# Six column orders for the up products of the third expert in a two-layer hybrid block with a mixture of experts

## The chip, the cores and the metric

The kernel runs on one core of one Trainium2 chip. The metric is the device time of one execution in microseconds (us); the median over the runs is what counts. Beside it there is one profiled execution, whose trace is read below. PE is TensorE (PEld its weight loads), DVE VectorE, ACT ScalarE, POOL GpSimd, SP SyncE, whose queue issues the loads.

## The reference, cut to what matters

Two layers of a mixer (gated convolution and chunkwise retention) and a feed-forward part, on 256 tokens of 1024 features. In the first layer the feed-forward part is dense, in the second it is a mixture of eight experts, two for each token, with 3584 inner features. The change is in the experts:

```python
def expert_block(args):
    xe, e = args
    a = xe @ w1[e]
    c = xe @ w3[e]
    return (jax.nn.silu(a) * c) @ w2[e]
```

All arrays are float32.

## The kernel before

After the mixer of the second layer the kernel gathers, for each expert, up to 128 of its tokens (a loop behind a condition serves more) and runs through the weights of all eight experts, 56 blocks in all: expert `e` from 0 to 7, and in it block `b` from 0 to 6, each block 512 of the 3584 inner features. The third expert is `e == 2`.

The float32 products are made of three products each. `parts` (L106 to L110) splits a weight half of 128 partitions x 1024 columns into a rounded high part `wh` (ACT, L109) and the remainder `wl` (DVE or POOL, L110); the tokens are split likewise (`gah` and `gal` for the third expert). `mm3` (L152 to L156) issues the three matmuls high by high (L154), high by low (L155) and low by high (L156), all into the same PSUM tile. Its first operand, the tokens, is loaded into the array (128 x 128, a weight load on PEld); its second, the weights of the expert, streams through as 512 columns, and the 512 results of each partition go to one bank of PSUM.

In a block the up products come first: four calls of `up` make `a` (the product with w1) and four more make `cc` (with w3). One call takes a half unit of weights, views it as two pieces of 512 columns, and calls `mm3` for each. So a block has 8 x 2 x 3 = 48 up matmuls: 24 into one tile `ac`, 24 into another. Between them stand the four transposes of the block before (`ph`, L816) and, in some blocks, small matmuls that gather tokens (`pg`) or scatter results (`pc`). Behind the up products come 24 down matmuls of the block before (`y`). `act` (L806 to L811) reads the two `ac` tiles, in plain order, in the next block.

The weights come through SP's queue in pieces of 1 MB (`raw`, L132), which wait for a free buffer; ACT and DVE split them into four pairs of `wh` and `wl`, which in turn come free when PE has used them. On each engine the instructions run in the order in which the program issues them.

Of the kernel before, what the change touches and what calls it, by code (L numbers as in the profile page):

```python
# [74 lines left out]
def tile_hybrid(ctx: ExitStack, tc, xT_in, x_in, ws, wm, cols, lnp, gnp, router, ident_in, rot, mask_in, out):  # L75
    nc = tc.nc
    v, sc, pe, gp = nc.vector, nc.scalar, nc.tensor, nc.gpsimd
    A = slice(None)
# [22 lines left out]
    def half(h):  # L101
        return slice(512 * h, 512 * h + 512)
# [43 lines left out]
    W = Stream(emit)  # L146
# [5 lines left out]
    def mm3(o, a, b, first, last):  # L152

        pe.matmul(o, a[0], b[0], start=first, stop=False, skip_group_check=True)  # L154
        pe.matmul(o, a[0], b[1], start=False, stop=False, skip_group_check=True)  # L155
        pe.matmul(o, a[1], b[0], start=False, stop=last, skip_group_check=True)  # L156

    def two(p, *idx):
        return (p[0][idx], p[1][idx])

    def view(p, pattern, **kw):
        return [w.rearrange(pattern, **kw) for w in p]


    for l in range(DEPTH):
        b = l * MIXU
# [60 lines left out]
    for q in range(4):  # L227
        k = slice(2 * q, 2 * q + 2)
# [489 lines left out]
    def bc(a):  # L718
        return a.unsqueeze(2).to_broadcast([128, NT, NE])
# [69 lines left out]
    def start_acc():  # L789

        for t in range(NT):
            for h in range(2):
                o = acc[:, t, half(h)]
                sc.mul(o, f32(xn[0][:, t, half(h)]), ALPHA)
                v.scalar_tensor_tensor(o, f32(xn[1][:, t, half(h)]), ALPHA, o, op0=ALU.mult, op1=ALU.add)
                yield

    def up(p, q, w, G):

        w = view(w, "p (k f) -> p k f", k=2)  # L800
        for k in range(2):
            mm3(p, two(G, A, 2 * q + k), two(w, A, k), q == 0 and k == 0, q == 3 and k == 1)

    def new_ac():
        return pac.tile([128, 512], F32, tag="ac", name="ac")

    def act(a, cc):
        hh = mo2.tile([128, 512], F32, tag="hh", name="hh")
        sc.activation(hh, a, AF.Silu)
        v.tensor_tensor(hh, cc, hh, op=ALU.mult)  # L810
        return hh  # L811

    def turn(hh):
        p = ptp.tile([128, 4, 128], F32, tag="tp", name="ph")
        for j in range(4):
            pe.transpose(p[:, j, :], hh[:, 128 * j:128 * j + 128], ident)  # L816
        return p

    def split_h(p):
        return split([128, 4, 128], p, mo2, "ht")  # L820
# [8 lines left out]
    got = {}  # L829
# [9 lines left out]
    def later_tokens(e0):  # L839
        g = tokens_of(e0)  # L840
        yield
        yield
        yield from g
# [20 lines left out]
    def step():  # L864
        while side:
            if next(side[0], 0) is None:
                return
            side.pop(0)
# [3 lines left out]
    def down_prev(last):  # L872
        nonlocal y, hT
        hp = hT
        pe_, pb, _ = prev
        if pb == 0:
            y = new_y()
        for q in range(4):
            down(hp, q, W.take(), y, pb == 0, pb == NB - 1)
            if q == 0:  # L880
                step()
            if last and q == 1:
                hT = [raw2[1 + i].tile([128, 4, 128], F32R, tag="raw", name="htl") for i in range(2)]
                parts(hT[0], hT[1], turn(hh))
        if pb == NB - 1:
            side.append(combine(y, got[pe_][1], lambda t: gate[:, t, pe_:pe_ + 1]))

    for e, b in blocks:
        if e == 0 and b == 1:
            W.look = LOOK  # L890
        if e == 1 and b == 0:
            assert main not in seq
            once.release()
            acc = main.tile([128, NT, D], F32, tag="x", name="acc")
            side.append(start_acc())
            late.append(ctx.enter_context(tc.tile_pool(name="late", bufs=1, reuse_waits="tile")))
        if e == 0 and b == 2:

            g = mo.tile([128, 4, NT], F32, name="g")
            v.tensor_tensor(g[:, 0], m2, m1, op=ALU.subtract)  # L900
            sc.activation(g[:, 1], g[:, 0], AF.Exp)
            v.tensor_scalar(g[:, 0], g[:, 1], 1.0, None, op0=ALU.add)
            v.reciprocal(g[:, 2], g[:, 0])
            v.tensor_tensor(g[:, 3], g[:, 1], g[:, 2], op=ALU.mult)
            gate = mo.tile([128, NT, NE], F32, name="gate")
            v.tensor_tensor(gate, s1, bc(g[:, 2]), op=ALU.mult)
            v.tensor_tensor(s2, s2, bc(g[:, 3]), op=ALU.mult)
            v.tensor_tensor(gate, gate, s2, op=ALU.add)
        if e % 2 == 1 and b == 2 and e + 1 < NE:
            side.append(later_tokens(e + 1))  # L910
        a = new_ac()
        for q in range(4):
            up(a, q, W.take(), got[e][0])
            if not prev:
                next(g0, 0), next(g0, 0)
            if prev and q == 0:
                hh = act(*prev[2])
            if prev and q == 2:
                hp = turn(hh)
            if prev and q == 3:  # L920
                hT = split_h(hp)
        step()
        cc = new_ac()
        for q in range(4):
            up(cc, q, W.take(), got[e][0])
            if q < 3:
                step()
        step()
        if prev:
            last = (e, b) == blocks[-1]  # L930
            if last:
                hh = act(a, cc)
            down_prev(last)
        prev = (e, b, (a, cc))
# [22 lines left out]
    for h in range(2):  # L957
        for t in range(NT):
            o = acc[:, t, half(h)]
# [20 lines left out]
    if GENERAL:  # L980
        most = nc.values_load(cnti[0:1, 0:1], min_val=0, max_val=S)
        with tc.If(most > WIN):
            rk2 = mo.tile([128, NT, NE], F32, name="rk2")
            v.tensor_scalar(rk2, rk, -float(WIN), None, op0=ALU.add)
            with tc.For_i(0, NE, 1) as e:
                rc = mo.tile([128, NT, 2], F32, name="rc")
                for t in range(NT):
                    v.tensor_copy(rc[:, t, 0:1], rk2[:, t, ds(e, 1)])
                    v.tensor_copy(rc[:, t, 1:2], gate[:, t, ds(e, 1)])
                gg = gather(lambda i, t: rc[:, t, 0:1], 1, ((mo, "ga"),), mo)  # L990
                gs, PT = next(gg)
                run(gg)
                yy = new_y()
                for b in range(NB):
                    def src(i):
                        return wm[ds(e, 1), 6 * b + i].rearrange("o p f -> (o p) f")

                    def both(i):
                        s = Unit(src(i))
                        return [emit("first", s), emit("second", s)]  # L1000

                    ac = [new_ac(), new_ac()]
                    for i in range(4):
                        for j, w in enumerate(both(i)):
                            up(ac[i // 2], 2 * (i % 2) + j, w, gs[0])
                    hT = split_h(turn(act(*ac)))
                    for i in range(2):
                        for j, w in enumerate(both(4 + i)):
                            down(hT, 2 * i + j, w, yy, b == 0, b == NB - 1)
                run(combine(yy, PT[:, 0, :], lambda t: rc[:, t, 1:2]))  # L1010
# [5 lines left out]
    for t in (1, 0):  # L1016
        for h in range(2):
            o = acc[:, t, half(h)]
            v.scalar_tensor_tensor(o, o, mv[:, t, 0:1], gt[:, 0, half(h)], op0=ALU.subtract, op1=ALU.mult)  # L1019
    for t, h in ((1, 0), (1, 1), (0, 0), (0, 1)):  # L1020
        o = acc[:, t, half(h)]
# [92 lines left out]
```

## Time and profile before

| what | value |
|---|---|
| median of the runs | 1468.6 us (two runs, 1467.22 and 1469.97) |
| the profiled execution | 1474.45 us, its span 1472.6 us |
| granted PE clock, mean | 0.986 |
| PE busy | 1436.3 us, 98% of the span |
| DVE busy | 1226.3 us, 83% |
| ACT busy | 973.6 us, 66% |
| DMA | 77.5% of 16 engines' span, 295 GB/s of reads and writes |

The span is what the trace covers, and 1.85 us lie around it. A busy share counts an instruction from its start to its end, and matmuls overlap: one of 512 columns is drawn 0.39 us long, but the next starts after some 0.23 us. So PE's time is read from the distance between starts.

### The profile page before, as it was taken

The page shows a single profiled execution, that of the slowest core. Times are in us where ns is not written, and L with a number is a line of the kernel's source. Part 1 is how long each engine was busy: PE and PEld are TensorE (multiplying, and loading weights), DVE is VectorE, ACT ScalarE, POOL GpSimd, SP SyncE. Part 2 cuts the span into 40 slices and gives each one's busy share as a digit, 9 for nine tenths or more (in the row PEclk, how much of TensorE's full clock was granted, in tenths as well). Part 3 has the DMA queues.
Part 4 walks back from the last instruction along what each step waited for, and adds up shares of the span by engine and source line. Part 5 has one row for each costly group of instructions (what it writes and reads, how often), then busy time and mean ns, then how long its engine had stood idle before and what let it go on. Part 6 is the DMA issues. An engine that isn't in the chain of part 4 may idle for free. (4 is left out here: it accounts for less than half of the span.)

```text
span 1472.6 us, 19730 instructions
## 1 busy us (share of the span) xinstructions
PE 1436.3 (98%) x7385; PEld 1211.4 (82%) x7385; DVE 1226.3 (83%) x1405; ACT 973.6 (66%) x1155; POOL 269.6 (18%) x136
## 2 busy tenths in 40 slices
PE   9999999999997999999999999999999999999995
PEld 8859999999866888888888888888888888888884
DVE  7976545547996799999999998999999899999996
ACT  6324444443524787877778777887887777778773
POOL 5630000001844111111111111111111111111111
PEclk9999999999997999999999999999999999999998
DMA  9535454454637879998999998999999899999951
GB/s 367 215 115 217 183 195 178 180 192 160 219 114 286 344 283 361 369 356 341 378 356 378 365 359 332 365 364 372 378 367 346 336 374 352 375 367 369 369 209 60
DMA packets 62311, 436.10 MB, mean 296 GB/s; under 512 B 7040, under 2 KB 7424, under 8 KB 9856
## 3 DMA queue, kind: packets, MB, share of 16 engines
q1 hardware_dynamic: 61920, 434.24, 77.5%
q8 instruction: 60, 0.98, 0.3%
q10 hardware_dynamic: 288, 0.52, 0.1%
q14 instruction: 43, 0.35, 0.1%
HBM read 433.69 MB, written 1.05 MB: 295 GB/s over the span
## 5 line engine op out<-in xcount | busy, mean ns | idle before, releaser
L110 DVE TENSOR_TENSOR wl<-raw,wh 128x1024 fp32r<-128x1024 f32 (+1 forms) x704 | 880.0, 1285 | 60.6 <-ACT wh L109 37.3
L109 ACT CAST wh<-raw 128x1024 fp32r<-128x1024 f32 (+1 forms) x802 | 822.0, 1046 | 155.1 <-PE ac L156 90.0
L110 POOL TENSOR_TENSOR wl<-raw,wh 128x1024 fp32r<-128x1024 f32 x98 | 242.3, 2488 | 1095.1 <-ACT wh L109 1019.4
L154 PE MATMUL ac<-wh,gah 128*128 128x512 f32 x448 | 177.4, 396 | 0.0
L155 PE MATMUL ac<-wl,gah 128*128 128x512 f32 x448 | 174.9, 390 | 0.5 <-POOL wl L110 0.5
L156 PE MATMUL ac<-wh,gal 128*128 128x512 f32 x448 | 175.0, 391 | 0.0
L156 PE MATMUL y<-wh,htl 128*128 128x512 f32 x448 | 174.4, 389 | 0.0
L155 PE MATMUL y<-wl,hth 128*128 128x512 f32 x440 | 171.7, 390 | 0.1
L154 PE MATMUL y<-wh,hth 128*128 128x512 f32 x440 | 171.4, 389 | 0.0
L154 PE MATMUL wk<-xh,wh 128*128 128x256 f32 x512 | 145.6, 284 | 0.7 <-ACT wh L109 0.7
L156 PE MATMUL wk<-xh,wl 128*128 128x256 f32 x512 | 145.1, 283 | 0.0
L155 PE MATMUL wk<-xl,wh 128*128 128x256 f32 x512 | 144.9, 283 | 0.0
L391 DVE SCALAR_TENSOR_TENSOR wk<-u,colt,wk 128x256 f32<-128x256 f32 x209 | 99.8, 488 | 5.7
L156 PEld LDWEIGHTS wk<-xh,wl 128*128 128x128 f32 x512 | 99.2, 194 | 0.5 <-DVE wl L110 0.5
L154 PEld LDWEIGHTS wk<-xh,wh 128*128 128x128 f32 x512 | 97.5, 190 | 2.4 <-ACT wh L109 1.3
L155 PEld LDWEIGHTS ac<-wl,gah 128*128 128x128 f32 x448 | 84.4, 188 | 17.7 <-POOL wl L110 0.9
L156 PEld LDWEIGHTS ac<-wh,gal 128*128 128x128 f32 x448 | 84.2, 188 | 17.9
L155 PEld LDWEIGHTS wk<-xl,wh 128*128 128x128 f32 x512 | 97.6, 191 | 0.9
L156 PEld LDWEIGHTS y<-wh,htl 128*128 128x128 f32 x448 | 84.1, 188 | 17.4
L154 PEld LDWEIGHTS ac<-wh,gah 128*128 128x128 f32 x448 | 84.5, 189 | 16.6
L155 PEld LDWEIGHTS y<-wl,hth 128*128 128x128 f32 x440 | 82.6, 188 | 18.8 <-DVE wl L110 1.9
L154 PEld LDWEIGHTS y<-wh,hth 128*128 128x128 f32 x440 | 82.6, 188 | 17.1
(202 smaller groups left out, 2049.6 us busy)
## 6 DMA issues: line engine op xcount, KB each, us to landing
raw<-in_wm_dram SPq DMA_DIRECT2D x336, 1024.0 KB, 6.6
raw<-in_ws_dram SPq DMA_DIRECT2D x68, 1024.0 KB, 4.9
raw<-in_lnp_dram SPq DMA_DIRECT2D x4, 1024.0 KB, 4.6
raw<-in_ws_dram SPq DMA_DIRECT2D x8, 256.0 KB, 5.7
xf<-in_xT_dram SPq DMA_DIRECT2D x4, 256.0 KB, 4.9
x<-in_x_dram SPq DMA_DIRECT2D x1, 1024.0 KB, 7.4
mask<-in_mask_dram SPq DMA_DIRECT2D x1, 768.0 KB, 12.1
gn<-in_gnp_dram SPq DMA_DIRECT2D x2, 256.0 KB, 8.3
```

The costliest lines, as they stand in the source:

```text
L109: sc.copy(hi, src)
L110: (eng or v).tensor_tensor(lo, src, f32(hi), op=ALU.subtract)
L154: pe.matmul(o, a[0], b[0], start=first, stop=False, skip_group_check=True)
L155: pe.matmul(o, a[0], b[1], start=False, stop=False, skip_group_check=True)
L156: pe.matmul(o, a[1], b[0], start=False, stop=last, skip_group_check=True)
L391: v.scalar_tensor_tensor(d, u[:, cc, k:k + S], w[:, k:k + 1], o, op0=ALU.mult, op1=ALU.add)
```

## The change

In blocks 1 to 6 of the third expert the streamed operand and the PSUM output of all 48 up matmuls are addressed through the same rearranged pattern. Each column still meets its own place in PSUM, so the tile `ac` holds what it held; only the order in time in which the 512 columns pass is another. Block 0 and all other experts keep the plain order.

```diff
+    walks = (None, ("p (a b i) -> p b a i", dict(a=2, i=2)), ("p (a b i) -> p b a i", dict(a=32, i=2)),
+             ("p (c a i) -> p a c i", dict(a=2, i=16)), ("p (a i) -> p a i", dict(a=4)),
+             ("p (a b i) -> p b a i", dict(a=2, i=16)), ("p (a b i) -> p b a i", dict(a=4, i=4)))
+
+    def walk(o, n):
+
+        return o.rearrange(walks[n][0], **walks[n][1]) if walks[n] else o
+
-    def up(p, q, w, G):
+    def up(p, q, w, G, n=0):
 
         w = view(w, "p (k f) -> p k f", k=2)
         for k in range(2):
-            mm3(p, two(G, A, 2 * q + k), two(w, A, k), q == 0 and k == 0, q == 3 and k == 1)
+            mm3(walk(p, n), two(G, A, 2 * q + k), [walk(o, n) for o in two(w, A, k)], q == 0 and k == 0, q == 3 and k == 1)
...
-            up(a, q, W.take(), got[e][0])
+            up(a, q, W.take(), got[e][0], b if e == 2 else 0)
...
-            up(cc, q, W.take(), got[e][0])
+            up(cc, q, W.take(), got[e][0], b if e == 2 else 0)
```

The six orders, in columns of 4 bytes:

| block | shape of the walk | adjoining columns in a row | from there it goes | stretches in 512 columns |
|---|---|---|---|---|
| 1 | 128 x 2 x 2 | 2 | to and fro between the two halves, 256 columns apart | 256 |
| 2 | 8 x 32 x 2 | 2 | 16 columns on from the last start | 256 |
| 3 | 2 x 16 x 16 | 16 | 32 columns on, then once more for the other half of each 32 | 32 |
| 4 | 4 x 128 | 512 | nowhere: this is the plain order | 1 |
| 5 | 16 x 2 x 16 | 16 | to and fro between the two halves | 32 |
| 6 | 32 x 4 x 4 | 4 | 128 columns on, four such places in turn | 128 |

No instruction is added, removed or moved. On PE, where the down products `y` of block 0's turn end and the up products of block 1 begin, the kernel before has these rows:

```order
L155 MATMUL y<-wl,hth 128x512
L156 MATMUL y<-wh,htl 128x512
L154 MATMUL ac<-wh,gah 128x512
L155 MATMUL ac<-wl,gah 128x512
L156 MATMUL ac<-wh,gal 128x512
```

and the changed one these:

```order
L155 MATMUL y<-wl,hth 128x512
L156 MATMUL y<-wh,htl 128x512
L154 MATMUL ac<-wh,gah 128x128x2x2
L155 MATMUL ac<-wl,gah 128x128x2x2
L156 MATMUL ac<-wh,gal 128x128x2x2
```

The shapes (partitions first, then the walk) are all that differs. The same holds in blocks 2, 3, 5 and 6 with the shapes of the table. In block 4 PE's rows in the changed kernel are those of before, the four pieces of 128 columns having been merged into one run of 512:

```order
L155 MATMUL y<-wl,hth 128x512
L156 MATMUL y<-wh,htl 128x512
L154 MATMUL ac<-wh,gah 128x512
L155 MATMUL ac<-wl,gah 128x512
L156 MATMUL ac<-wh,gal 128x512
```

So five blocks of 48 matmuls, 240 in all, have another order.

## Rows read from the trace of the kernel before

**Rows 1.** The profile's page: the span, the engines' busy time, slices in tenths
```profile
span 1472.6 us, 19730 instructions
PE 1436.3 (98%) x7385; PEld 1211.4 (82%) x7385; DVE 1226.3 (83%) x1405; ACT 973.6 (66%) x1155; POOL 269.6 (18%) x136
PE   9999999999997999999999999999999999999995
PEclk9999999999997999999999999999999999999998
```

**Rows 2.** Busy time by stretch: expert 3's blocks 1 to 6, one row each
```profile
core 0: us, PE busy (x) PEld busy (x) DVE busy (x) ACT busy (x) POOL busy (x), PEclk, DMA share, GB/s
737.26:754.98 17.72, 17.72 (x82) 14.66 (x80) 17.05 (x17) 14.18 (x17) 2.40 (x1) 1.00 0.90 331
754.98:772.68 17.70, 17.70 (x82) 14.66 (x80) 16.74 (x16) 13.39 (x15) 2.50 (x1) 1.00 0.96 376
772.68:789.49 16.81, 16.81 (x77) 13.90 (x76) 15.27 (x13) 13.40 (x15) 2.42 (x1) 1.00 0.96 376
789.49:806.28 16.79, 16.79 (x77) 13.91 (x76) 15.26 (x13) 13.39 (x15) 2.42 (x1) 1.00 0.94 375
806.28:823.10 16.82, 16.82 (x78) 13.91 (x76) 15.26 (x13) 13.41 (x15) 2.41 (x1) 1.00 0.95 373
823.10:839.89 16.79, 16.79 (x77) 13.91 (x76) 15.26 (x13) 13.40 (x15) 2.42 (x1) 1.00 0.96 376
```

**Rows 3.** Waits in expert 3 (720.47 to 839.89): us in total, times, longest
```profile
POOL wl L110 <- ACT wh L109: 102.5, 7, 15.3
ACT wh L109 <- PE ac L156: 12.8, 40, 0.8
ACT wh L109 <- PE y L156: 6.9, 21, 0.8
```

**Rows 4.** The same stretch, SP's queue of loads
```profile
SPq L132 <- DVE wl L110: 104.8, 43, 3.7
```

**Rows 5.** Timeline of PE, block 5's up products: start, length, instruction
```profile
806.28 0.39 PE L154 MATMUL ac<-wh,gah 128*128 128x512 f32 x1
806.51 0.39 PE L155 MATMUL ac<-wl,gah 128*128 128x512 f32 x1
...
810.14 0.39 PE L156 MATMUL ac<-wh,gal 128*128 128x512 f32 x1
810.37 0.60 PE L816 MATMUL ph<-ident,hh 128*128 128x128 f32 x4
810.72 0.48 PE L154 MATMUL ac<-wh,gah 128*128 128x512 f32 x1
```

**Rows 6.** Timeline of PE, products of 256 columns in the dense layer
```profile
199.75 0.28 PE L154 MATMUL wk<-xh,wh 128*128 128x256 f32 x1
...
203.52 0.28 PE L156 MATMUL wk<-xh,wl 128*128 128x256 f32 x1
```

**Rows 7.** Timeline of PE, the first up products of the first expert
```profile
479.69 0.63 PE L154 MATMUL ac<-wh,gah 128*128 128x512 f32 x1
480.11 0.63 PE L155 MATMUL ac<-wl,gah 128*128 128x512 f32 x1
480.54 0.63 PE L156 MATMUL ac<-wh,gal 128*128 128x512 f32 x1
480.97 0.47 PE L154 MATMUL ac<-wh,gah 128*128 128x512 f32 x1
```

**Rows 8.** Busy time by stretch: the three matmuls ahead of 480.97 us
```profile
479.69:480.97 1.28, 1.28 (x5) 0.99 (x5) 0.70 (x2) 0.56 (x2) 0.00 (x0) 0.50 0.98 416
```

**Rows 9.** Groups by line, shapes apart: count, busy us, mean ns, idle before
```profile
L421 DVE TENSOR_TENSOR u<-wk,sgl 128x256 f32<-128x256 f32 x8 | 3.4, 419 | 3.3 <-ACT sgl L420 3.3
L441 DVE TENSOR_TENSOR t<-wk,rott 128x256 f32<-128x256 f32 x8 | 3.0, 414 | 0.0
L110 DVE TENSOR_TENSOR wl<-raw,wh 128x1024 fp32r<-128x1024 f32 x692 | 872.2, 1295 | 59.2 <-ACT wh L109 35.9
L109 ACT CAST wh<-raw 128x1024 fp32r<-128x1024 f32 x790 | 815.2, 1052 | 153.3 <-PE ac L156 90.0 <-PE y L156 48.7 <-PE wk L156 12.3
```

## The prediction, made before the changed kernel ran

> **What bounds the kernel now.** I began with the page: PE is busy 98% of the span and its row of tenths falls below 9 only around the start of the experts and in the last slice, and the clock's row with it [rows 1]. A busy share proves little for matmuls that overlap, so I looked at the six blocks by stretch: PE has work in every microsecond of all of them, at a granted clock of 1.00 [rows 2]. Next, who waits for whom in this expert: ACT's splitting waits for PE to give back weights, POOL waits for ACT, SP's queue of loads waits 104.8 us for buffers that the splitting gives back, and no row has PE waiting for anything [rows 3, 4]. So the weights are there before PE wants them; the feed follows PE, not the reverse, though DMA at a share of 0.90 to 0.96 is near its own limit. Last, PE's timeline: in block 5 the starts of 18 up matmuls go from 806.28 to 810.14 us, 17 steps of 0.2271 us each, and after the four transposes the next 30 follow at the same pace [rows 5]. PE sets the time here and nothing behind it is slack: a microsecond that an up matmul gains or loses is a microsecond of the kernel.
>
> **The change part by part.** Nothing is moved, added or waited for anew. Weight loads are the same instructions, the tile `ac` has the same content, and its readers read it in plain order. Blocks 0 and 4 are as before. What is left is one question: how long 512 columns take in five orders, for 48 matmuls each.
>
> What a column costs in plain order comes from two rows. Products of 256 columns start 32 steps apart between 199.75 and 203.52 us, 0.1178 us each [rows 6]. From 256 to 512 columns the step grows by 0.1093 us, that is 0.427 ns a column, and some 8 ns of a step are fixed.
>
> The trace has no matmul whose streamed operand or output hops, so the price is bounded from both sides.
>
> *From below:* a walk cannot stream faster than one column at a time, so a gain could come from the fixed 8 ns alone, 240 x 8 ns = 1.9 us; nothing in the change touches them, and I take 0.
>
> *From above, for a walk at half pace:* at a granted clock of 0.50 [rows 8], the lower of the two levels (1.2 GHz), the first three up matmuls of the first expert start 0.4267 us apart, (480.97 - 479.69) / 3 [rows 7]. That is 512 columns at half pace, and 0.1996 us more than at 1.00. For the five orders together: 240 x 0.1996 = 47.9 us.
>
> Which of the five pay? The nearest row with hops is on DVE: L441 (in `rotary`) reads PSUM and writes its result in pieces of 32 elements with 32 left out between them, and takes 414 ns for 256 elements, against 419 ns for L421, which reads and writes in one run [rows 9]. Hops between long pieces are free there. But DVE and ACT are slow readers: 1295 ns and 1052 ns for 1024 elements, 1.26 and 1.03 ns each [rows 9], while PE draws one every 0.427 ns, two and a half to three times as many. What hides a hop there may not here. And 16 adjoining columns (walks 3 and 5, one hop in 6.8 ns) are near that row, 2 adjoining columns (walks 1 and 2, one hop in 0.85 ns) are far from it; 4 (walk 6, one in 1.7 ns) lie between.
>
> I think of it as a fetch that brings a few adjoining columns at once at a steady rate that the plain order just uses up. Nothing here shows how many. If two, every walk is free. If four, walks 1 and 2 need twice the fetches (256 for 128) and run at half pace, the others are untouched. If eight, they run at a quarter and walk 6 at half. I take four: the plain order needs no more than one fetch in 1.7 ns then, close to the 1.03 to 1.26 ns at which the other engines take even a single element, while two would mean a fetch in 0.85 ns, faster than any row shows.
>
> **The sum.** 96 matmuls (walks 1 and 2) x 0.1996 us = 19.2 us. The profiled execution would go from 1474.45 to 1493.6 us (its span from 1472.6 to 1491.8). The median of the runs lies 5.85 us below that execution, so I forecast 1468.6 + 19.2 = 1487.8 us, 1.3% longer. Nothing gives it back: the loads were already waiting for buffers, so a slower PE lets no work run ahead that PE later saves.
>
> [...]
>
> **The rivals.**
>
> *All walks are free* (fetches of two columns, or more fetches at hand than the plain order uses): 1468.6 us, not slower. For it speaks L441; against it that PE draws 2.5 times as fast. It decides wherever the extra is under 0.03 us a matmul.
>
> *Any stepped pattern runs at half pace,* long pieces too, for instance because the output side takes two results at once only in plain order: 240 x 0.1996 = 47.9 us, 1516.5 us, 3.3% slower. Against it speaks L441 for the reading; for writing to PSUM at this pace no row speaks at all. The line to slower by over 2% (29.4 us) lies at 29.4 / 240 = 0.122 us a matmul if all five pay alike, or 0.306 us if walks 1 and 2 pay alone. [...]
>
> *Short pieces cost far more* (fetches of eight columns): walks 1 and 2 at a quarter pace take twice the 0.4267 us of half pace [rows 7], 0.8534 - 0.2271 = 0.6263 us more than now, times 96 that is 60.1 us; walk 6 at half pace adds 48 x 0.1996 = 9.6 us: 1468.6 + 69.7 = 1538.3 us. Against it: a fetch would then take 3.4 ns, while ACT takes single elements in 1.03 ns each [rows 9].
>
> *Faster:* 1.9 us at most, so not by 2%.
>
> **How the numbers follow.** The likeliest, walks 1 and 2 at about half pace, has 0.38; its own range is 1478 (only one of them pays, 9.6 us) to 1498 (a third order or a second hop cost joins, 28.8 us). All free has 0.35. All five at half pace has 0.13, far more for short pieces 0.12, and 0.02 is left for a time a little below that of before. The range takes in the first three: 1465 us (the free case less the 1.9 us and the 1 to 2 us by which the runs differ) to 1517 us, leaving out the dear short pieces, 0.12, and what is left. About 2% is what a measurement of this kernel can tell from no change. Slower by over 2%: 0.13 + 0.12 and 0.02 from the upper edge of the likeliest, 0.27. Within 2%: 0.72. Faster: 0.01.
>
> **What would show it.** In the trace after, each block is its own experiment. Steps between starts of `ac` matmuls: 0.227 us in blocks 0 and 4; 0.43 us in blocks 1 and 2, which then last 17.7 + 9.6 = 27.3 us; 0.227 us in blocks 3, 5 and 6, which stay at 16.8 us. ACT's waits for PE `ac` grow by about what PE loses, the granted clock stays at 1.00, and no row of PE waiting appears. A step of 0.227 us in blocks 1 and 2 makes the first rival true; over 0.3 us in block 3 or 5 makes the second; 0.6 us and more in block 1 or 2 the third. A cost in one of blocks 1 and 2 alone would mean that the distance of the hop counts, not only the length of the piece. What makes the forecast wrong is the choice of four columns a fetch, which no row settles.

## The result and the profile after

The changed kernel takes 1487.6 us (two runs, 1487.18 and 1488.02) against 1468.6 us: 1.0131 times the time before, with a 95% interval of 1.0107 to 1.0156. That is 19.0 us more, where 19.2 were forecast. The sum came out, in part by luck: of its terms one was 4.5 us too high, and three that it put at nothing make 3.2 us.

The profile's page of the changed kernel, with the lines that answer to [rows 1]:

```profile
span 1485.4 us, 19726 instructions
PE 1448.2 (97%) x7385; PEld 1207.8 (81%) x7385; DVE 1227.4 (83%) x1405; ACT 974.0 (66%) x1155; POOL 269.3 (18%) x136
PEclk9999999999998999999999999999999999999998
```

Nothing in it tells what happened: PE's share is a point lower, the clock is where it was. The stretches tell it. These are the six blocks of expert 3, as in [rows 2] (stretch, its length, then busy time of PE, PEld, DVE, ACT, POOL, granted clock, DMA share, GB/s):

```profile
732.04:754.88 22.84, 22.84 (x81) 15.08 (x80) 18.10 (x17) 14.36 (x17) 2.39 (x1) 1.00 0.80 288
754.88:782.45 27.57, 27.57 (x81) 15.52 (x80) 17.09 (x15) 13.45 (x15) 2.39 (x1) 1.00 0.62 222
782.45:799.84 17.39, 17.39 (x78) 13.94 (x76) 15.44 (x13) 13.38 (x15) 2.40 (x1) 1.00 0.95 357
799.84:816.64 16.80, 16.80 (x78) 13.91 (x76) 15.25 (x13) 13.40 (x15) 2.41 (x1) 1.00 0.95 368
816.64:834.09 17.45, 17.45 (x78) 14.02 (x77) 15.44 (x13) 13.39 (x15) 2.40 (x1) 1.00 0.97 374
834.09:852.87 18.78, 18.78 (x78) 14.24 (x77) 15.49 (x13) 13.71 (x15) 2.36 (x1) 1.00 0.90 335
```

Against 17.72, 17.70, 16.81, 16.79, 16.82 and 16.79 us before [rows 2], the blocks grew by 5.12, 9.87, 0.58, 0.01, 0.63 and 1.99 us, 18.20 in all. (The medians, of two runs each, differ by 19.0; the runs of the kernel before alone lie 2.75 us apart.) PE is busy in every microsecond of them, and the clock stays at 1.00. Behind block 6 both profiled executions run alike: 1485.4 - 852.87 = 632.5 us here, 1472.6 - 839.89 = 632.7 before. Ahead of block 1 this execution was 5.2 us quicker (732.04 for 737.26), in parts that the change doesn't touch; that is why the spans differ by 12.8 only and the medians by 19.0.

The timeline of PE gives the step, from the first to the 18th `ac` matmul of a block (17 steps), here of blocks 1, 2, 3 and 6:

```profile
732.04 0.50 PE L154 MATMUL ac<-wh,gah 128*128 128x512 f32 x1
...
737.80 0.52 PE L156 MATMUL ac<-wh,gal 128*128 128x512 f32 x1
...
754.88 0.59 PE L154 MATMUL ac<-wh,gah 128*128 128x512 f32 x1
...
762.20 0.62 PE L156 MATMUL ac<-wh,gal 128*128 128x512 f32 x1
...
782.45 0.41 PE L154 MATMUL ac<-wh,gah 128*128 128x512 f32 x1
...
786.54 0.40 PE L156 MATMUL ac<-wh,gal 128*128 128x512 f32 x1
...
834.09 0.43 PE L154 MATMUL ac<-wh,gah 128*128 128x512 f32 x1
...
838.64 0.44 PE L156 MATMUL ac<-wh,gal 128*128 128x512 f32 x1
```

That is 0.3388, 0.4306, 0.2406 and 0.2676 us, and 0.2400 in block 5, against 0.2265 in block 4, which keeps the plain order. All steps below are read in this way.

The waits of expert 3 from its block 0 on (715 to 852.87 us; us in total, times, longest) show where a slower PE is felt, as in [rows 3]:

```profile
POOL wl L110 <- ACT wh L109: 118.8, 7, 25.2
ACT wh L109 <- PE ac L156: 28.0, 43, 2.0
```

ACT waits 28.0 us for PE to release weights, 12.8 before; PE itself still has no row of waiting for the feed there.

### The profile page after: what moved, and what is told of

The parts are those of the page before. It is cut to its first block, busy times and chain, and to the rows that moved or that the text cites. A ratio compares the mean times of both kernels' runs of the same rounds, so it can differ in the third digit from the quotient of the medians.

```text
span 1485.4 us, 19726 instructions
## 1 busy us (share of the span) xinstructions
PE 1448.2 (97%) x7385; PEld 1207.8 (81%) x7385; DVE 1227.4 (83%) x1405; ACT 974.0 (66%) x1155; POOL 269.3 (18%) x136
## 5 line engine op out<-in xcount | busy, mean ns | idle before, releaser
L154 PE MATMUL ac<-wh,gah 128*128 128x512 f32 x448 | 183.5, 410 | 0.0
L155 PE MATMUL ac<-wl,gah 128*128 128x512 f32 x448 | 181.2, 404 | 0.5 <-POOL wl L110 0.5
L156 PE MATMUL ac<-wh,gal 128*128 128x512 f32 x448 | 181.4, 405 | 0.0
```

## The experiments

The first question was which side pays, the reading of the streamed operand or the writing of PSUM; the next which property of an order sets the price; the last whether an order can be quicker than the plain one.

**The operand alone.** `up` walks the operand as in the change and writes the output plainly. The table of walks has an entry for each block, first the operand's walk, then the output's (from the edit against the kernel before):

```diff
+    walks = {(2, 1): ((2, 2), None), (2, 2): ((32, 2), None), (2, 3): (("step", 2, 16), None), (2, 5): ((2, 16), None), (2, 6): ((4, 4), None)}
...
+            mm3(walk(p, n[1]), two(G, A, 2 * q + k), [walk(o, n[0]) for o in two(w, A, k)], q == 0 and k == 0, q == 3 and k == 1)
```

> The five walks on the streamed operand alone; the output is written in plain order, so in these five blocks the columns of a and cc change places and all else is as before. Theory O (the cost is in reading the streamed operand from SBUF): the steps between starts stay those of the changed kernel, 0.333 us in block 1, 0.431 in block 2, 0.241 in blocks 3 and 5, 0.268 in block 6; expert 3's blocks 1 to 6 last 120.8 us and the kernel some 1487.6 us, 1.3% over the one before. Theory P (the cost is in writing PSUM): all steps 0.227 us, 102.6 us, 1468.6 us. Theory B (both pay, and the dearer one shows): some blocks keep their step and others fall to 0.227 us.

Measured: 1.0154 times the time before, interval 1.0095 to 1.0213 (median 1494.24 of four runs from 1487.39 to 1498.12). The six blocks as one stretch:

```profile
736.05:856.88 120.83, 120.83 (x466) 86.78 (x465) 96.80 (x84) 81.71 (x87) 14.34 (x6) 1.00 0.83 314
```

This is 120.83 us, to the hundredth what the changed kernel takes for them (852.87 - 732.04), with the same steps (block 1's is 0.3388 us by the reading used here, for the 0.333 of the expectation). The whole took longer than the changed kernel. In the profiled execution, 1491.24 us, nearly all of that lies ahead of block 1 (736.05 for 732.04): the clock of 400 to 480 us was 0.85 there, in the changed kernel's 0.89 (the two rows, in this order). For the other executions there is no trace, so where their time went is not shown.

```profile
400.00:480.00 80.00, 67.96 (x327) 52.20 (x326) 63.78 (x145) 28.48 (x50) 34.96 (x21) 0.85 0.54 208
```

```profile
400.00:480.00 80.00, 67.75 (x334) 51.33 (x333) 62.95 (x144) 30.16 (x54) 33.25 (x20) 0.89 0.55 213
```

**The output alone.** The reverse edit: the same five walks stand in the second place of each entry, as in `(2, 1): (None, (2, 2))`.

> The five walks on the PSUM output alone, the streamed operand is read in plain order; again the columns of a and cc change places in these blocks. Theory O: every step 0.227 us, the six blocks 102.6 us, the kernel 1468.6 us. Theory P: 0.333, 0.431, 0.241, 0.240, 0.268 us in blocks 1, 2, 3, 5, 6, the six blocks 120.8 us, the kernel some 1487.6 us. Theory B: the blocks that fell to 0.227 us with the operand alone keep their step here.

Measured: 0.9992 times, interval 0.9973 to 1.0011, and the stretch of the six blocks is that of before, 102.63 us:

```profile
732.58:835.21 102.63, 102.63 (x466) 84.93 (x464) 94.87 (x84) 81.20 (x87) 14.57 (x6) 1.00 0.95 364
```

Theory O holds: the whole price is in reading the streamed operand. Pairs scattered over a PSUM bank are written and added up at full pace (0.2265 us in blocks 1 and 2), and no block's step is above 0.2271.

**Many orders at once.** The table of walks is made longer, with an entry for each of blocks 1 to 6 of five experts, and `rearrange("p (a b i) -> p b a i", a=a, i=i)` for operand and output.

> Operand and output walk alike, as in the changed kernel, but with other orders in blocks 1 to 6 of experts 3 to 7, to see whether the number of stretches or the distance of the hop sets the price. Written (a, i): i adjoining columns, then a hop of 512/a columns, a places in turn. Expert 3: (2,2) (4,2) (8,2) (16,2) (32,2) (64,2), pairs with hops of 256 to 8 columns. Expert 4: (128,2), pairs 4 apart, then fours: (2,4) (4,4) (8,4) (16,4) (32,4). Expert 5: (64,4), then eights: (2,8) (4,8) (8,8) (16,8) (32,8). Expert 6: (2,16) (4,16) (16,16) (2,32) (2,64) (2,128). Expert 7: pairs, taken at a step of 4, 8, 16, 32 and 128 columns right through the 512, then begun anew (2, 4, 8, 16, 64 times), and fours at a step of 8. Theory N (one column's time, 0.417 ns, for every stretch, whatever the hop): all orders of pairs 0.333 us, fours 0.280, eights 0.253, sixteens 0.240, 32s 0.233, 64s 0.230; block 2's 0.431 us is then unexplained. Theory D (the distance decides: a hop of 16 columns, 64 bytes, or a small multiple of it meets the same place of a memory again): pairs 0.33 us at hops of 256 to 64 columns, 0.43 us at 16, and likewise at other small hops; fours and eights at a hop of 16 cost more than at a hop of 256. Theory F (the forecast's: fetches of four columns): pairs 0.43 us wherever the next pair isn't in the same four, fours and longer 0.227 us.

Steps in us, by length of the stretch and by hop (a hop of 256 columns has two places, 128 four, and so on):

| hop in columns | 256 | 128 | 64 | 32 | 16 | 8 | 4 |
|---|---|---|---|---|---|---|---|
| pairs | 0.3394 | 0.4447 | 0.4906 | 0.4506 | 0.4300 | 0.4606 | 0.4524 |
| fours | 0.2506 | 0.2676 | 0.2776 | 0.2459 | 0.2241 | 0.2312 | plain |
| eights | 0.2429 | 0.2306 | 0.2500 | 0.2306 | 0.2335 | plain | |
| sixteens | 0.2400 | 0.2318 | | 0.2406 | plain | | |

Stretches of 64 and 128 columns in turn from two places 256 apart took 0.2265 and 0.2271 us. Those of 32 took 0.2367 (12 steps, ahead of a matmul that comes late).

The last expert's orders turned out to be five of the same orders and one of the fours, written another way; they came out the same to 1 ns. Theory N falls (pairs aren't 0.333 us everywhere). Theory F, the forecast's, holds for pairs at six hops of seven, near twice 0.2265, and for longer stretches it misses up to some 0.05 us, which follow the hop by no law that we found. Two things it doesn't explain: pairs in turn from two places cost only 1.5 times, and fours at hops of 16 are quicker than the plain order.

**Places, alignment, single columns.** The operand alone, by hand-made patterns, lists of (step, count) from the outermost to the innermost: `bass.AP(tensor=o.tensor, offset=o.offset + n[0], ap=[o.ap[0]] + [list(d) for d in n[1]])`.

> The streamed operand alone takes other patterns in blocks 1 to 6 of experts 3 to 7, the output stays plain; the patterns repeat or leave out columns, so a and cc aren't the products there; 512 columns pass as before. Expert 3: pairs in turn from two places, D = 256, 128, 64, 16, 512, 260 columns apart, both moving on by two. Expert 4: each pair twice; pairs in turn from four places 256 and 128 apart; two places 8 apart; each pair twice at steps of four; plain order written as pairs. Expert 5: fours with hops of 16, from column 0, then from column 2; plain order from column 2; pairs with hops of 16 from column 2, then 0; fours of which each second starts in mid-four. Expert 6: fours with hops of 8, 12, 20, 24, 28, 32. Expert 7: every second column, then on; singles in turn from two places 256 apart; singles with hops of 32 and 128; plain order from column 4 and 16. Theory K (fetches of four columns, aligned, and one is still at hand if one other came between): two places 0.34 us at every D from 16 up, four places 0.43 to 0.49; each pair twice 0.227; fours from column 0 0.224, from column 2 0.43 or more, plain from column 2 0.227; every second column 0.227, singles with hops 0.8 and more. Theory W (walk 1 was cheap as its places lie 256 apart): D = 256 0.34 us, 128, 64, 16 0.44, 0.49, 0.43. Theory R (a price for each stretch, wherever it starts): fours from column 2 cost what those from column 0 cost.

For the single columns with hops the expectation names the counts, 32 and 128; their hops were 16 and 4 columns. Below, "a four" is four adjoining columns from a multiple of four on, and a pattern "opens" a four when it comes to one that isn't at hand from just before. The decisive pair of rows are fours with hops of 16, from column 0 and from column 2 (first and 18th matmul each):

```profile
1030.60 0.39 PE L154 MATMUL ac<-wh,gah 128*128 128x512 f32 x1
...
1034.41 0.40 PE L156 MATMUL ac<-wh,gal 128*128 128x512 f32 x1
...
1048.24 0.61 PE L154 MATMUL ac<-wh,gah 128*128 128x512 f32 x1
...
1055.84 0.63 PE L156 MATMUL ac<-wh,gal 128*128 128x512 f32 x1
```

0.2241 us from column 0, 0.4471 from column 2: the same stretches, hops and count, only that each now lies across two fours. Theory R falls. Fetches of four columns, 16 bytes, from a multiple of four on would give these two steps; that is an estimate from them, since no row shows a fetch.

Pairs in turn from two places cost 0.3388, 0.3394, 0.3388 and 0.3388 us at 256, 128, 64 and 512 columns and 0.3271, 0.3265 and 0.3265 at 16, 260 and 8, so Theory W falls as well: what matters is that there are two places. With four places it is 0.4447 at both distances. Fours with hops of 8, 12, 20, 24, 28 and 32 take 0.2335, 0.2282, 0.2700, 0.3129, 0.2335 and 0.2518 us; fours of which each second starts in mid-four take 0.2706.

A miss of Theory K: every second column was expected at 0.227 us and took 0.4524; it opens a new four every second column as pairs do, which had been overlooked. And single columns with hops of 16 and 4 take 0.4324 and 0.4588 us, no more than pairs, where 0.8 and more was expected: a price for each fetched four can't be the whole story. Each pair twice, expected at 0.227 us, takes 0.2265 at steps of four columns and 0.2159 at steps of two, and single columns in turn from two places 256 apart 0.2153 (the rows below): the last two are quicker than plain.

```profile
1343.22 0.38 PE L154 MATMUL ac<-wh,gah 128*128 128x512 f32 x1
...
1346.88 0.38 PE L156 MATMUL ac<-wh,gal 128*128 128x512 f32 x1
```

**Turns.** More patterns of this kind, with the operand alone.

> The streamed operand alone takes other patterns in blocks 1 to 6 of experts 3 and 4, the output stays plain, and a and cc aren't the products there; 512 columns pass. Expert 3: pairs in turn from two places 258 and 18 columns apart, so that the two places enter a new four at different turns; single columns in turn from four places 128 apart and from eight places 64 apart; each four twice; one four over and over. Expert 4: single columns in turn from two places 4, 16, 64, 128, 258, 260 columns apart. Theory G (columns pass in groups of four by their turn; a group costs twice when both its halves open a new aligned four, one new four in a group is hidden, and the last two fours are at hand): 258 and 18 cost 0.227 us, where 256 and 260 cost 0.339 and 0.327; two places of single columns 0.215 to 0.22 at 16, 64, 128, and some more at 258, where the halves of the groups open fours in other turns. Theory K2 (a price for each new four, whatever its turn): 258 and 18 cost 0.33 to 0.34 us. [...] Four places: 0.22 us if four fours are at hand, 0.43 or more if only two; eight places likewise.

258 and 18 columns apart cost 0.3306 and 0.3288 us, so Theory G (groups of four by their turn) falls. Four places of single columns take 0.2812 us, eight places 0.4906. Single columns in turn from places 4, 258 and 260 apart take 0.2159, 0.2165 and 0.2159 us. At 16, 64 and 128 a weight load waits once in each block for POOL's `wl` (1.5 us in all) and the matmul behind it comes late; the 12 steps ahead of that are 0.2158, 0.2150 and 0.2158 us.

Each four twice takes 0.2159 us, and so does one four over and over (the rows below):

```profile
854.01 0.38 PE L154 MATMUL ac<-wh,gah 128*128 128x512 f32 x1
...
857.68 0.38 PE L156 MATMUL ac<-wh,gal 128*128 128x512 f32 x1
```

At a granted clock of 0.50 a step of 512 columns took 0.4267 us [rows 7, 8]. Half of that, 0.2133 us, is an estimate of what the columns alone take at 1.00; no step of any run was under 0.2150. By this estimate 0.2159 - 0.2133 = 2.6 ns of a step are left in the quick patterns, and the other 10.6 ns of the plain step (0.2265 us) go with the order in which the operand is read. It seems not to be simply so much a column: the products of 256 columns [rows 6], with the tokens as the operand, stand 0.1178 - 0.1067 = 11.1 ns above theirs, nearly as much as the 13.2 of 512. No run changed the order of those, so this stays open.

**A rule, tried on new patterns.** A rule was read off these steps and then tried on six patterns that hadn't run.

> Six new patterns on the streamed operand alone in expert 3, the output plain; a and cc aren't the products there; 512 columns pass. They try a rule that was read off the earlier runs: the stream is drawn two columns a turn (0.833 ns); a turn that opens an aligned four takes two turns' time, one or two new fours alike, but the next turn rides along free if it stays in the fours just opened; a four is still at hand if one other turn's fours came between. With 2.6 ns fixed, a plain or better pattern gives 0.216 us and somewhat more by where the hops land. Block 1, fours with hops of 6: 1.5 times, 0.323 us. Block 2, eights with hops of 10: 1.25 times, 0.269. Block 3, single columns in turn from two places 256 apart, both moving on by two: 0.216 to 0.227 us. Block 4, the same, moving on by three: 1.5 times, 0.323. Block 5, each pair four times: 0.216. Block 6, fours with hops of 5, which start at odd columns too: 1.25 times, 0.269. The rival, a price for each four newly opened (128 of them are free, each more costs 1.67 ns): the same in blocks 1 and 2, but block 3 opens 256, 0.43 us, and block 4 384, 0.64 us.

Blocks 3 and 4, single columns in turn from two places, moving on by two and by three:

```profile
776.41 0.39 PE L154 MATMUL ac<-wh,gah 128*128 128x512 f32 x1
...
780.26 0.40 PE L156 MATMUL ac<-wh,gal 128*128 128x512 f32 x1
...
793.21 0.50 PE L154 MATMUL ac<-wh,gah 128*128 128x512 f32 x1
...
798.98 0.52 PE L156 MATMUL ac<-wh,gal 128*128 128x512 f32 x1
```

0.2265 and 0.3394 us, where the rival asked for 0.43 and 0.64. The other four took 0.3388, 0.2824, 0.2159 and 0.2859 us for 0.323, 0.269, 0.216 and 0.269. All six multiples come out. The sizes as recorded were 13 to 17 ns too low in the four patterns that pay; they come out to 3 ns if the multiple is taken of the plain step (1.5 x 0.2265 = 0.340, 1.25 x 0.2265 = 0.283), a choice made after the run.

The rule is an estimate from the steps above: the stream draws two columns a turn. A turn that opens an aligned four takes twice as long, one new four or two alike, unless the next turn stays in it and so rides along. A four is still at hand if one other turn came between. Plain order (0.2265 us) alternates, open and ride, and just keeps pace; pairs open at every turn (2 times; 0.4300 to 0.4906 us measured at the six hops that pay); pairs from two places open at two turns and then find both fours at hand (1.5 times; 0.3265 to 0.3394 us measured).

It describes steps and is no mechanism that a run has shown, and it doesn't cover all of them. Fours with hops of 64, 20 and 24 columns should keep the plain pace by it and took 0.2776, 0.2700 and 0.3129 us, and it has no reason why the plain order stands 10.6 ns above the quickest ones.

**Fours everywhere.** The first order that was quicker than plain, for all products of 512 columns: in `mm3`, `o, b = fours(o), [fours(w) for w in b]` with `rearrange("p (a b i) -> p b a i", a=32, i=4)`.

> All products of 512 columns, up and down and in the layers before, walk fours with hops of 16 columns (4 x 32 x 4), operand and output alike, because one block in which they did had steps of 0.2241 us against 0.2265 us in plain order. Theory S (the fixed part of a step is smaller in this order, everywhere): 56 blocks x 72 matmuls x 2.4 ns = 9.7 us, and some 720 matmuls of the layers before 1.7 us more: 1468.6 - 11.4 = 1457 us, 0.8% faster than before. Theory C (a chance of that block, its buffers or its feed): no change, 1468 us. Theory L (the feed then limits, DMA having been busy at a share of 0.90 to 0.96): less than 0.8%, and rows of PE waiting for weights appear.

Measured: 1461.46 us, 0.9947 times, interval 0.9924 to 0.9971. The gain is 8.5 us (1469.98 in the runs beside it) where 11.4 was expected. The interval leaves out 1, so Theory C falls as a whole, but it was half right about the block. From the third block of the experts to the start of the last, 53 blocks, the trace shows 915.37 us (500.34 to 1415.71), and 920.08 with the operand in plain order (505.73 to 1425.81, in the run of the output alone). That is 4.7 us, half of what 2.4 ns a matmul would give; the steps go from 0.2235 to 0.2276 us by block. The rest of the gain lies ahead of the experts, where executions differ by some 5 us anyway; its cause isn't shown. PE's waits for `wl` in the experts are 2.1 us (none of them from 700 to 840 us), 1.0 before: too little for Theory L.

**Two places in turn, everywhere.** By the rule the pattern with 0.2153 us opens two fours at one turn and then has three turns without. For the result to land in plain order, the weights lie dealt out in memory:

```diff
+    def turns(w):
+        return w.rearrange("p (a b) -> p b a", a=2)
...
+        b = [turns(w) for w in b] if b[0].shape[-1] == 512 else b
...
+def _turned(w):
+    return np.ascontiguousarray(w.reshape(w.shape[:-1] + (-1, 256, 2)).swapaxes(-1, -2)).reshape(w.shape)
...
-        "ws": c(ws), "wm": c(wm), "cols": c(col), "lnp": c(lnp), "gnp": c(gnp),
+        "ws": c(ws), "wm": _turned(wm), "cols": c(col), "lnp": c(lnp), "gnp": c(gnp),
```

This is the form for all products of 512 columns, where the weights of the mixers and the dense layer are dealt out likewise; for the experts alone `turns` stands in `up` and `down`.

> All up and down products of the experts draw single columns in turn from two places 256 columns apart (256 x 2 on the streamed operand, the output plain); the weights lie in memory with their 512 columns dealt out likewise, so the products are the same in plain order. Theory S (steps of 0.2153 us, as one block showed with this pattern, against 0.2265): 56 blocks x 72 x 11.2 ns = 45.2 us, 1468.6 - 45.2 = 1423 us, 3.1% faster. Theory L (the feed takes over as the bound: DMA stood at a share of 0.90 to 0.96 and DVE at 15.3 of 16.8 us a block): some of it, 1430 to 1460 us, with rows of PE waiting for wh or wl, and SP's waits for buffers much shortened. Theory C (the block's gain doesn't carry over): 1468 us.

> As the kernel with the experts' products in turns, and the 720 products of 512 columns of the mixers and the dense layer too (their weights laid out likewise). Theory S: 720 x 11.2 ns = 8.1 us more at most, 1415 us; where PE isn't what these stages wait for, less, down to the time of the experts alone.

Measured: the experts alone 1435.29 us, 0.9757 times (0.9739 to 0.9775); all of them 1428.45 us, 0.9721 times (0.9700 to 0.9742), 2.8% faster than the kernel before and the fastest that was run. A block's step is 0.2159 us (685.80 to 689.47, 17 steps):

```profile
685.80 0.38 PE L158 MATMUL ac<-wh,gbh 128*128 128x512 f32 x1
...
689.47 0.38 PE L160 MATMUL ac<-wh,gbl 128*128 128x512 f32 x1
```

The experts alone brought 34.9 us (1470.15 beside them) of the 45.2 expected: 56 x 72 x 10.6 ns is 42.7 (the step is 0.2159 us in most blocks, not 0.2153). Of the 7.8 us still missing most went to the feed, as Theory L said: in the trace of this run PE waits 7.8 us for `wl` in the experts (6.9 of them from 600 to 1400 us), and 1.0 in that of the kernel before, by the row below.

```profile
PE ac L155 <- POOL wl L110: 1.0, 4, 0.5
```

The mixers and the dense layer brought 6.8 us more, of 8.1 at most. The engines' line on the page of the fastest kernel, its stretch from 600 to 1000 us, and PE's waits in the experts for `wl` over the whole run:

```profile
PE 1379.5 (97%) x7385; PEld 1207.9 (85%) x7385; DVE 1220.9 (86%) x1405; ACT 970.5 (68%) x1155; POOL 274.5 (19%) x136
600.00:1000.00 400.00, 395.91 (x1897) 342.70 (x1897) 379.27 (x357) 321.32 (x357) 60.62 (x23) 1.00 0.96 371
PE ac L159 <- POOL wl L110: 5.1, 15, 0.7
PE y L159 <- DVE wl L110: 2.7, 5, 0.8
```

PE waits 7.8 us for `wl` here too and is idle for 4.1 of these 400 us, while DVE is busy 379.27. The feed is close to being the next bound, though it isn't yet.

## Why the prediction was right, and where it wasn't

**PE as the bound, one for one:** right. The blocks grew by 18.20 us, nothing behind them gave any of it back, and no wait of PE appeared in them.

**The price of half pace:** right. Walk 2 was put at 0.1996 us more a matmul and measured 0.4306 - 0.2265 = 0.2041; its block was to last 27.3 us and lasted 27.57.

**Fetches of four columns:** right as a choice. The sentence that chose four over two by comparison with the other engines' pace was weak grounds; the fours from column 0 (0.2241 us) and column 2 (0.4471) have since agreed with it.

**Walk 1 at half pace:** mis-sized, the term of 9.6 us measured 5.12. It supposed that each pair needs a fetch of its own. With two places in turn a step took 0.3388 us, 1.5 times the plain one and not twice; by the rule, an estimate, the second visit to a four finds it at hand. The forecast's sign that the hop's distance counts, a cost in one of walks 1 and 2 alone, doesn't describe this: both paid, by different amounts, and it is the number of places that matters. Pairs from two places took 0.327 to 0.339 us at all nine distances that were run.

**Walks 3, 5 and 6 at no cost:** too low, 0.58, 0.63 and 1.99 us. Fours and sixteens open no more fours than the plain order, but by the hop they take from 2 ns less to 86 ns more (0.2241 to 0.3129 us for 0.2265), for a reason that stays open. DVE's row L441, the grounds for putting them at nothing, gave no measure for 14 ns on PE.

So 19.2 was made of 9.6 + 9.6, and 18.20 of 5.12 + 9.87 + 0.58 + 0.63 + 1.99 + 0.01: 4.5 too much in one term, 3.2 too little in three and 0.3 too little in walk 2. That these nearly cancel was luck; the terms as measured make 18.2.

**Some 8 ns of a step fixed, and a gain of 1.9 us at most:** wrong, and the step of the working that mattered most for what came after. The slope between 256 and 512 columns (0.427 ns) was taken for the pace of the array, though half of the 0.4267 us that 512 columns took at a granted clock of 0.50 [rows 7, 8] is only 0.4167 ns each. By this estimate no more than 2.6 ns are left in the quickest patterns (0.2153 to 0.2159 us); 10.6 ns of each plain step can be saved by order. The prediction's 1.2 GHz is these 512 columns over 0.4267 us, 1.2 columns a ns; the profile gives the granted clock as a share alone.

**The rivals.** All free: no, pairs with hops took 1.4 to 2.2 times the plain step (0.3265 to 0.4906 us for 0.2265). All five at half pace: no, sixteens cost 6% (0.2400 and 0.2406 us in blocks 5 and 3), and the output in the same orders nothing. Dear short pieces: no, pairs took at most 2.2 times the plain step (0.4906 us), and single columns with hops of 16 about what pairs took (0.4324 us for 0.4306).

## What to carry to other kernels

Where PE is the bound, give its streamed 4-byte operand stretches of at least four columns that start at a multiple of four (0.2241 us from column 0, 0.4471 from column 2, at hops of 16 columns), and time the hop, since fours took from 0.2241 to 0.3129 us by it. The order of the output in PSUM was free for pairs, fours and sixteens (102.63 us for the six blocks, with it and without); single columns weren't tried on it. Taking the columns singly in turn from two places, with the weights laid out for it, beat the plain order by 10.6 ns for each matmul of 512 columns and this kernel by 2.8%. And look at what a step takes above half of its time at a granted clock of 0.50: of that remainder, 13.2 ns here, 10.6 were not fixed.

## What the runs showed of the hardware that was not expected

The plain order isn't the quickest: 0.2265 us for 512 columns against 0.2153 to 0.2159 where, by the rule, a four, once opened, serves for three turns more. Single columns from two places 256 apart (0.2153 us) are as good as one four drawn over and over (0.2159). Pairs, fours and sixteens written to PSUM in the orders of the change cost nothing (steps of 0.2265 to 0.2271 us). Left open: why fours take from 0.2241 us (hops of 16 columns) to 0.3129 (hops of 24), and why the plain order takes 0.2335 us from column 2, 0.2318 from column 4 and 0.2300 from column 16.
